# Seven-product pairs in half of the second feed-forward's down projections

## The chip, the core and the metric

The kernel runs on one core of a Trainium2 chip. Five engines work side by side, each through its own list of instructions in order: TensorE (PE: matmuls; the loading of its stationary operand is shown as PEld), VectorE (DVE), ScalarE (ACT), GpSimd (POOL) and SyncE (SP), which here only issues transfers. Engines wait for each other through semaphores. The metric is the time of one execution on the device, in microseconds; the kernel before takes 2179.33 us (median of three runs, 2179.05 to 2179.38).

## The reference

One decoder layer on 256 tokens with 16 learned tokens ahead of them, model width 2048, all in float32. The part that is changed is the last one:

```
gate, up = split(rms_norm(s) @ w_gu)          # 2048 -> 2 x 5632
s = s + 0.5 * ((silu(gate) * up) @ w_down)    # 5632 -> 2048, the "down projection"
out = rms_norm(s)[:, 16:]
```

`w_down` is 5632 x 2048. Ahead of this stand a first feed-forward of the same kind, an attention branch and a convolution branch with gates, and an output projection.

## The kernel before

**Split operands.** Each float32 operand of a matmul is made into two parts of the type float32r: `hi`, a rounded copy made on ACT, and `lo`, the rest, made on DVE by a subtraction. A product of two operands is three matmuls, hi x hi, lo x hi and hi x lo. For weights the parts are called `wh` and `wl`. `parts` (L407) makes them: a cast on ACT at L420 and a subtraction on DVE at L421, for 128x1024 (a tile) or 128x512 elements. PE reads `wl` only in the third matmul of a product. A tile's buffers, `wh` and `wl`, come from three each (`W_BUFS`), so a tile can be split as soon as the third tile before it has been used. A 512-wide tile takes two buffers of another pair, "sc", which has two.

**Order of the work.** `step` (L252) holds each tile's matmuls back until `AHEAD` = 2 more tiles have had their splitting written down. So in DVE's list the splits of the next two tiles stand ahead of the steps that evict a finished sum. The final order on each engine is made by a planner, which keeps to this order where the operands allow it and fills gaps with later work; buffers of one pool go to tiles in the order in which the program names them. Three lists carry side work: `pending` (evictions, run by `flush`), `later` (the `back` steps) and `side` (other small jobs); stages pop them at fixed tiles.

**Two ways of a matrix product.** `linear_tok` (L345) multiplies 256 tokens (two halves, i) by 1024 columns (two blocks of 512, q), going through the rows of the weight in chunks of 128: 2 x 2 products of three matmuls, 12 per chunk, 24 per pair of chunks, into four accumulators. `linear_mix` (L498) goes through pairs of chunks, with a letter for each in its plan. A D pair is as in `linear_tok`: 24 matmuls into the accumulators 2, 3, 4 and x. An S pair does the same 2x2 block product with seven products in place of eight (Winograd's form of Strassen's scheme): 21 matmuls into the accumulators 1 to 7. For that it needs sums of blocks of the weight (`sums`, L550: t13 by one 128x1024 addition at L553, t24 by two 128x512 additions at L554 and L555), and four sums of blocks of the activation, split into parts (`combine`, L483). t13 can also be made by two transfers, the second of which adds (`prefetch`, L559, issued by POOL at L563 and L564); the pairs for which that is done are the fourth entry of a plan. The third entry says after which tile the weight sums of which pair are made; the second entry is the pair at which `later` is popped. The result has to be put together from the seven accumulators when they are finished (`done`).

**The second feed-forward.** The 5632 inner columns are 11 groups of 512. They are done in thirds of 4, 4 and 3 groups. In each third, `gate_up_mix` makes the group's gate and up columns by `linear_mix` (plan `FFN2`, "DDSDSSDS", for the first group `FFN2_FIRST`) and turns the product with four PE transposes per `back` step (L647) into the activation `m`, already split. Then the down projection of this third's rows adds to `sT`, the residual, kept by token, in two stages of 1024 columns: u=0 and u=1. Both are `linear_tok`, of 16 chunks in the first two thirds and 12 in the last. Their four accumulators are evicted at the second chunk of the next stage by L1058, which halves and adds. In the last third the eviction also squares and sums each row (L1062) and multiplies by the last norm's gain (L1064); the very last stage holds back the second token half of its last six chunks (`HOLD`), so that the first half can be finished early.

**Buffers that the change touches.** `aux` has three buffers. The gate/up groups use them for t13 (`prefetch` into them runs ahead as far as they are free); the branch gates' stage (plan `GATES`, "DDDSDSDS", no t13 by transfer) holds its activation sums in them.

The accumulators lie in eight banks. Weights come on SP's queue into four staging buffers `st`, 1 MB for a pair.

Of the kernel before, what the change touches and what calls it, by code (L numbers as in the profile page):

```python
# [22 lines left out]
GC = 4  # L23
GW = GC * P
W2 = D // 2
# [14 lines left out]
HOLD = 6  # L40
# [3 lines left out]
GATES = ("DDDSDSDS", 2, {(2, 1): 3, (4, 1): 5, (6, 1): 7}, ())  # L44
FFN2_FIRST = ("DDDDSSDS", 1, {(3, 0): 4, (3, 1): 5, (6, 0): 7}, (4, 5))
FFN2 = ("DDSDSSDS", 1, {(1, 1): 2, (3, 0): 4, (3, 1): 5, (6, 0): 7}, (2, 4, 5))
AHEAD = 2


@with_exitstack  # L50
def decoder_layer(ctx: ExitStack, tc: tile.TileContext, t, out):
    nc = tc.nc
# [11 lines left out]
    def wide(shape, name):  # L64
        return tmp.tile(shape, F32, tag="wide", bufs=4, name=name)
# [16 lines left out]
    x = t["x"][0]  # L82
# [25 lines left out]
    def load_vectors():  # L108
# [12 lines left out]
        out=mask[:, T - P :],  # L121
# [330 lines left out]
    class Mixed:  # L452
# [22 lines left out]
        def sum(self, p):  # L475
# [4 lines left out]
                nc.vector.tensor_scalar_mul(f[:, k, :], s(c, NMETA), col(self.g0 + c))  # L480
            self.combine(p, f)

        def combine(self, p, f):  # L483
            a11, a12, a21, a22 = (f[:, c, i * P : (i + 1) * P] for i in range(2) for c in range(2))
            q = tmp.tile([P, 4, P], F32, tag="sc", name="sums")
            nc.vector.tensor_sub(q[:, 0, :], a21, a22)
            nc.vector.tensor_sub(q[:, 1, :], q[:, 0, :], a11)
            nc.vector.tensor_sub(q[:, 2, :], a11, a21)
            nc.vector.tensor_add(q[:, 3, :], a12, q[:, 1, :])
            sp = (aux if self.in_aux else apool).tile([P, 4, 2, P], F32R, tag="act", name=f"sp{p}")  # L490
            nc.scalar.copy(out=sp[:, :, 0, :], in_=q)
            nc.vector.tensor_sub(sp[:, :, 1, :], q, sp[:, :, 0, :].bitcast(F32))
            self.sums[p] = [[sp[:, k, lo, :] for lo in range(2)] for k in range(4)]
# [4 lines left out]
    def linear_mix(plan, a, w, cols, name, done):  # L498

# [36 lines left out]
        def load(p):  # L536

            st = wpool.tile([P, 2, 2, GW], F32, tag="st", bufs=ST_BUFS, name="st")
            rows = w[2 * p * P : (2 * p + 2) * P, :].rearrange("(c p) f -> p c f", p=P)
            for q in range(2):  # L540
                nc.sync.dma_start(out=st[:, :, q, :], in_=rows[:, :, cols[q] : cols[q] + GW])
            if kinds[p] == "S":
                if not by_load:
                    t13s[p] = wpool.tile([P, 2, GW], F32, tag="tt", bufs=2, name="t13")
                elif p not in by_load:
                    t13s[p] = aux.tile([P, 2, GW], F32, tag="act", name="t13")
                t24s[p] = wpool.tile([P, 2, GW], F32, tag="tt", bufs=2, name="t24")
            return st
# [176 lines left out]
    for half in halves:  # L725
# [288 lines left out]
    def finish_part(i):  # L1014

        nc.vector.tensor_reduce(out=fr[:, i, 3:4], in_=fss[:, i, 0:3], axis=AX.X, op=ALU.add)
        nc.vector.tensor_scalar(fpart[:, i : i + 1], fr[:, i, 3:4], 1.0 / D, EPS, op0=ALU.mult, op1=ALU.add)

    def finish(i, last):

        ms, a, r, n = (fr[:, i, k : k + 1] for k in range(4))
        nc.vector.tensor_scalar(ms, fss[:, i, 3:4], 1.0 / D, fpart[:, i : i + 1], op0=ALU.mult, op1=ALU.add)
        nc.scalar.activation(a, ms, AF.Sqrt)
        nc.vector.reciprocal(r, a)
        nc.vector.scalar_tensor_tensor(out=n, in0=r, scalar=ms, in1=r, op0=ALU.mult, op1=ALU.mult)
        nc.vector.tensor_scalar(n, n, -0.5, 1.5, op0=ALU.mult, op1=ALU.add)
        nc.vector.tensor_mul(a, r, n)
        rows = out[i * P : (i + 1) * P, :]
        for u, q in ((0, 1), (0, 0), (1, 0), (1, 1)) if i else ((0, None), (1, None)):
            cs = slice(0, W2) if q is None else slice(q * GW, (q + 1) * GW)  # L1030
            on_act = q == 0 or (q is None and u == 0)
            y = last if u and q else sT[i][u][:, cs]
            if on_act:
                nc.scalar.mul(y, y, a)
            else:
                nc.vector.tensor_scalar(y, y, r, n, op0=ALU.mult, op1=ALU.mult)
            eng = nc.scalar if on_act and i else nc.sync
            eng.dma_start(out=rows[:, u * W2 + cs.start : u * W2 + cs.stop], in_=y)

    w_gu, w_down = t["ffn2_w_gu"][0], t["ffn2_w_down"][0]  # L1040
    thirds = [list(range(0, 4)), list(range(4, 8)), list(range(8, ng))]
    for half in thirds:
        m = Act("m", len(half) * GC, SEQ)
        for gi, g in enumerate(half):
            gate_up_mix(FFN2 if g else FFN2_FIRST, hn, norm3, w_gu, g, m, gi)
        final = half is thirds[-1]
        if final:
            for q in range(2):
                nc.gpsimd.dma_start(
                    out=gfin[q],  # L1050
                    in_=t["norm_final"][q * W2 : (q + 1) * W2].rearrange("(o d) -> o d", o=1).to_broadcast([P, W2]),
                )
        for u in range(2):

            def down(i, q, ps, u=u, final=final):
                fs = slice(q * GW, (q + 1) * GW)
                v = sT[i][u][:, fs]
                nc.vector.scalar_tensor_tensor(out=v, in0=ps, scalar=0.5, in1=v, op0=ALU.mult, op1=ALU.add)  # L1058
                if final:
                    k = u * 2 + q  # L1060
                    sq = wide([P, GW], "fsq")
                    nc.scalar.activation(sq, v, AF.Square, accum_out=fss[:, i, k : k + 1])  # L1062
                    y = wide([P, GW], "fy") if k == 3 and i else v
                    nc.vector.tensor_mul(y, v, gfin[u][:, fs])  # L1064
                    if k == 1 and i:

                        nc.scalar.activation(fr[:, i, 3:4], fss[:, i, 1:2], AF.Sqrt)
                    if k == 2:
                        finish_part(i)
                    if k == 3:  # L1070
                        finish(i, y)

            hold = HOLD if final and u else 0
            linear_tok(
                [(m, 0, w_down, u * W2 + q * GW) for q in range(2)], list(range(len(half) * GC)), half[0] * GC, "pd",
                down if hold else lambda acc, down=down: [down(i, q, acc[i][q]) for q in range(2) for i in range(2)],
                hold=hold,
            )
    drain()


# [23 lines left out]
```

## Time and profile before

The profiled execution took 2179.22 us, of which the instructions span 2177.4. Its engines:

| | busy us | share of the span |
|---|---|---|
| PE matmuls | 2166.5 | 99% |
| weight loads (beside PE) | 1966.7 | 90% |
| DVE | 1485.7 | 68% |
| ACT | 1060.8 | 49% |
| POOL | 64.8 | 3% |

The stretches of the second feed-forward, by where the product names on PE change (us from the span's start):

| stretch | from | to | us |
|---|---|---|---|
| first third, down u=0 | 1635.71 | 1680.20 | 44.49 |
| first third, down u=1 | 1680.20 | 1723.72 | 43.52 |
| fifth gate/up group | 1723.72 | 1765.30 | 41.58 |
| second third, down u=0 | 1890.04 | 1934.53 | 44.49 |
| second third, down u=1 | 1934.53 | 1978.06 | 43.53 |
| last third, down u=0 | 2102.57 | 2136.18 | 33.61 |
| last third, down u=1, up to where `HOLD` works off its last block | 2136.18 | 2168.86 | 32.68 |

How to read the lines in this document: a timeline row is start, duration, engine, line of the kernel, operation, result<-operands, shape; "[1.20 <-ACT wh L420]" is idle time of that engine just before, and what ended it. "pd" are the down projection's accumulators, "pg" and "g" those of the gate/up groups and the branch gates, "t" the sums of weights, "sums" and "sp" those of the activation, "mt_ps" and L652 the transposes of `back`. A stretch's row gives its length, then the busy time of PE, PEld, DVE, ACT and POOL, the granted clock of PE, the share of the transfer engines and GB/s.

### The profile page before, as it was taken

The numbers are of one execution on the slowest core, as the hardware profiler recorded it, in microseconds if no ns is written. First come the engines' busy times: TensorE is split into PE (matmuls) and PEld (weight loads), VectorE is DVE, ScalarE is ACT, GpSimd is POOL, SyncE is SP. The second block draws the span as 40 slices with busy tenths as digits, with TensorE's granted clock in tenths as the row PEclk, the third lists the DMA queues.
The fourth block names the chain that finished last, engine by engine and source line by source line (L and its number), as shares of the span: only waits on it lengthen the run. The fifth ranks groups of instructions, "written<-read, shape, count | busy, mean of one in ns | idle before, by whom it ended". The sixth has DMA issues, their size and how long they took to land.

```text
span 2177.4 us, 33253 instructions
## 1 busy us (share of the span) xinstructions
PE 2166.5 (99%) x13489; PEld 1966.7 (90%) x13489; DVE 1485.7 (68%) x1942; ACT 1060.8 (49%) x1333; POOL 64.8 (3%) x73
## 2 busy tenths in 40 slices
PE   9999999999999999999999999999999999999998
PEld 9999999999999999999988888888888888888886
DVE  8555554445555555567897778678996599957985
ACT  6343343343433444444555555456664466534654
POOL 0000000000000000000000000001110011100100
PEclk9999999999999999999999999999999999999999
DMA  7555555555555555444555556557887589866973
GB/s 254 174 175 175 174 178 174 175 175 175 175 175 173 175 175 185 162 154 139 173 186 204 191 201 224 194 191 241 265 271 234 190 280 278 272 209 207 288 241 116
DMA packets 206432, 435.52 MB, mean 200 GB/s; under 512 B 10237, under 2 KB 10950, under 8 KB 206278
## 3 DMA queue, kind: packets, MB, share of 16 engines
q1 hardware_dynamic: 192214, 398.13, 53.4%
q0 software_dynamic: 13600, 34.61, 6.8%
q8 instruction: 105, 1.72, 0.3%
q10 hardware_dynamic: 464, 0.66, 0.1%
q14 instruction: 49, 0.40, 0.1%
HBM read 431.26 MB, written 2.10 MB: 199 GB/s over the span
## 4 chain that ended last, share of the span: by engine, by line
PE 98%; DVE 1%; ACT 0%; DMA 0%; issue 0%; SPq 0%; DVEq 0%
PE pg L518 6%; PE pg L519 6%; PE pg L520 6%; PE pd L320 4%; PE pu L320 4%; PE pd L318 4%; PE pu L318 4%; PE pu L319 4%; PE pd L319 4%; PE pg L320 4%; PE pg L318 4%; PE pg L319 4%; PE pd L360 4%; PE pd L359 4%; PE pd L358 4%; PE o L316 3%
## 5 line engine op out<-in xcount | busy, mean ns | idle before, releaser
L307 DVE TENSOR_TENSOR wl<-st,wh 128x1024 fp32r<-128x1024 f32 (+1 forms) x393 | 479.4, 1221 | 439.5 <-ACT wh L302 438.7
L302 ACT CAST wh<-st 128x1024 fp32r<-128x1024 f32 (+1 forms) x392 | 410.7, 1048 | 604.0 <-PE pd L319 147.3
L421 DVE TENSOR_TENSOR wl<-st,wh 128x1024 fp32r<-128x1024 f32 (+1 forms) x360 | 408.6, 1140 | 132.4 <-ACT wh L420 130.9
L420 ACT CAST wh<-st 128x1024 fp32r<-128x1024 f32 (+1 forms) x360 | 347.6, 986 | 260.6 <-PE pd L359 121.3
L318 PE MATMUL pg<-h,wh 128*128 128x272 f32 x704 | 203.2, 289 | 1.0 <-ACT h L190 0.7
L318 PE MATMUL pu<-h,wh 128*128 128x272 f32 x704 | 203.1, 289 | 0.0
L318 PE MATMUL pd<-m,wh 128*128 128x272 f32 x704 | 203.1, 288 | 0.0
L320 PE MATMUL pd<-m,wl 128*128 128x272 f32 x704 | 203.0, 288 | 0.0
L320 PE MATMUL pu<-h,wl 128*128 128x272 f32 x704 | 203.0, 288 | 0.0
L319 PE MATMUL pu<-h,wh 128*128 128x272 f32 x704 | 202.4, 288 | 0.0
L319 PE MATMUL pd<-m,wh 128*128 128x272 f32 x704 | 202.4, 288 | 0.0
L319 PE MATMUL pg<-h,wh 128*128 128x272 f32 x704 | 201.9, 288 | 0.1
L320 PE MATMUL pg<-h,wl 128*128 128x272 f32 x704 | 201.1, 289 | 0.3
L420 ACT CAST wh<-t 128x1024 fp32r<-128x1024 f32 x110 | 115.3, 1052 | 145.0 <-DVE t L555 82.9
L421 DVE TENSOR_TENSOR wl<-t,wh 128x1024 fp32r<-128x1024 f32 x110 | 134.2, 1223 | 37.7 <-ACT wh L420 32.8
L519 PE MATMUL pg<-wh,h 128*128 128x512 f32 x399 | 156.3, 392 | 0.0
L520 PE MATMUL pg<-wl,h 128*128 128x512 f32 x399 | 156.1, 391 | 0.0
L518 PE MATMUL pg<-wh,h 128*128 128x512 f32 x399 | 155.7, 390 | 0.0
L358 PE MATMUL pd<-wh,m 128*128 128x512 f32 x352 | 137.5, 391 | 0.0
L360 PE MATMUL pd<-wl,m 128*128 128x512 f32 x352 | 137.1, 389 | 0.0
L359 PE MATMUL pd<-wh,m 128*128 128x512 f32 x352 | 137.0, 389 | 0.0
L318 PEld LDWEIGHTS pg<-h,wh 128*128 128x128 f32 x704 | 132.3, 188 | 1.9 <-ACT h L190 0.9
(297 smaller groups left out, 4787.7 us busy)
## 6 DMA issues: line engine op xcount, KB each, us to landing
st<-in_ffn_w_gu_dram SPq DMA_DIRECT2D x183, 512.0 KB, 5.4
st<-in_ffn_w_down_dram SPq DMA_DIRECT2D x88, 1024.0 KB, 5.1
st<-in_ffn_w_gu_dram SPq DMA_DIRECT2D x84, 1024.0 KB, 4.9
st<-in_w_in_dram SPq DMA_DIRECT2D x48, 1024.0 KB, 5.1
st<-in_w_gate_dram SPq DMA_DIRECT2D x64, 512.0 KB, 4.3
t<-in_ffn_w_gu_dram POOLq DMA_DIRECT2D x64, 512.0 KB, 7.4
st<-in_w_branch_dram SPq DMA_DIRECT2D x32, 512.0 KB, 4.9
st<-in_w_out_dram SPq DMA_DIRECT2D x16, 1024.0 KB, 5.1
```

The costliest lines, as they stand in the source:

```text
L302: nc.scalar.copy(out=wh[:, :m, :], in_=sw)
L307: nc.vector.tensor_sub(wl[:, :m, :], sw, wh[:, :m, :].bitcast(F32))
L318: nc.tensor.matmul(a, wh[:, i, f], act.part(c, 0, t0, t1), start=first, stop=False)
L319: nc.tensor.matmul(a, wh[:, i, f], act.part(c, 1, t0, t1), start=False, stop=False)
L320: nc.tensor.matmul(a, wl[:, i, f], act.part(c, 0, t0, t1), start=False, stop=last)
L358: nc.tensor.matmul(ps, hi, wh[:, q, :], start=first, stop=False)
L360: nc.tensor.matmul(ps, hi, wl[:, q, :], start=False, stop=last)
L420: part_last[:] = [nc.scalar.copy(out=wh, in_=src).ins]
L421: part_last.append(nc.vector.tensor_sub(wl, src, wh.bitcast(F32)).ins)
L518: nc.tensor.matmul(ps[k], hi, wh, start=first, stop=False)
L519: nc.tensor.matmul(ps[k], lo, wh, start=False, stop=False)
L520: nc.tensor.matmul(ps[k], hi, wl, start=False, stop=left[k] == 0)
```

## The change

In one column half of each third the down projection goes by `linear_mix`, with S pairs.

- First two thirds: u=1 by `down_mix` with the plan `DOWN`, "DDSDSDSD": S pairs 2, 4 and 6 of 8. u=0 stays `linear_tok`, but at its chunks 3, 7 and 11 the sums of the activation for the pairs 2, 4 and 6 are made (`sum_of_parts`: hi and lo are added back together, then `combine`), into the three `aux` buffers.
- Last third: u=0 by `down_mix` with the plan `DOWN_LAST`, "DDDSDS": S pairs 3 and 5 of 6; their activation sums are made in the same stage, behind pairs 0 and 1, and the `back` steps of the last group at pair 1. u=1 stays `linear_tok` with `HOLD`.
- `t13` is made on DVE in both plans. The weight of a pair is loaded by one transfer, as in `linear_tok`.
- Evictions come as soon as an accumulator is finished, by the new `done`. In the last third squares and gain products (`score`) are made behind them, at the second chunk of u=1.

```diff
+DOWN = ("DDSDSDSD", None, {(1, 1): 2, (3, 1): 4, (5, 1): 6}, ())
+DOWN_LAST = ("DDDSDS", 1, {(2, 1): 3, (4, 1): 5}, ())
...
+        def sum_of_parts(self, p):
+
+            f = tmp.tile([P, 2, SEQ], F32, tag="sc", name="mf")
+            hi, lo = (self.act.tiles[p][:, :, k, :].bitcast(F32) for k in range(2))
+            nc.vector.tensor_add(f, hi, lo)
+            self.combine(p, f)
...
-            rows = w[2 * p * P : (2 * p + 2) * P, :].rearrange("(c p) f -> p c f", p=P)
-            for q in range(2):
-                nc.sync.dma_start(out=st[:, :, q, :], in_=rows[:, :, cols[q] : cols[q] + GW])
+            rows = w[(k0 + 2 * p) * P : (k0 + 2 * p + 2) * P, :].rearrange("(c p) f -> p c f", p=P)
+            if cols[1] == cols[0] + GW:
+                nc.sync.dma_start(out=st.rearrange("p c q f -> p c (q f)"), in_=rows[:, :, cols[0] : cols[0] + 2 * GW])
+            else:
+                for q in range(2):
+                    nc.sync.dma_start(out=st[:, :, q, :], in_=rows[:, :, cols[q] : cols[q] + GW])
...
+    def down_mix(plan, a, w, k0, u, end):
+        v = [[sT[i][u][:, q * GW : (q + 1) * GW] for q in range(2)] for i in range(2)]
+        ev = {}
+
+        def half_of(ps, out_, other, op1=ALU.add, by=0.5):
+            nc.vector.scalar_tensor_tensor(out=out_, in0=ps, scalar=by, in1=other, op0=ALU.mult, op1=op1)
+
+        def done(k, ps):
+            if k == "1":
+                ev["p1"] = wide([P, 2, GW], "dp")
+                nc.scalar.mul(ev["p1"][:, 0, :], ps, 0.5)
+                nc.vector.tensor_add(v[0][0], v[0][0], ev["p1"][:, 0, :])
+            elif k == "6":
+                half_of(ps, ev["p1"][:, 0, :], ev["p1"][:, 0, :])
+                nc.vector.tensor_add(v[1][0], v[1][0], ev["p1"][:, 0, :])
+            elif k == "5":
+                e = ev["p1"][:, 1, :]
+                half_of(ps, e, ev["p1"][:, 0, :], ALU.subtract)
+                for i in range(2):
+                    nc.vector.tensor_add(v[i][1], v[i][1], e)
+            elif k == "7":
+                half_of(ps, v[1][0], v[1][0])
+                half_of(ps, v[1][1], v[1][1], by=-0.5)
+            else:
+                i, q = {"2": (0, 0), "3": (0, 1), "4": (1, 0), "x": (1, 1)}[k]
+                half_of(ps, v[i][q], v[i][q])
+            ev[k] = True
+            if all(n in ev for n in "1234567x"):
+                pending.append(end)
+
+        linear_mix(plan, a, w, (u * W2, u * W2 + GW), "pd", done, k0)
...
+            if final and u == 0:
+                side.append(lambda: None)
+                side.extend(lambda p=p: ma.sum_of_parts(p) for p in (3, 5))
+                down_mix(
+                    DOWN_LAST, ma, w_down, half[0] * GC, u,
+                    lambda score=score: [score(i, q) for q in range(2) for i in range(2)],
+                )
+            elif u == 0:
+                side.append(lambda: None)
+                side.extend(lambda p=p: ma.sum_of_parts(p) for p in (2, 4, 6))
+                linear_tok(
+                    ops, chunks, half[0] * GC, "pd",
+                    lambda acc, down=down: [down(i, q, acc[i][q]) for q in range(2) for i in range(2)],
+                    side_at=(3, 7, 11),
+                )
+            elif not final:
+                down_mix(DOWN, ma, w_down, half[0] * GC, u, lambda: None)
+            else:
+                linear_tok(ops, chunks, half[0] * GC, "pd", down, hold=HOLD)
```

`score` is the part of the old `down` that followed the eviction (L1059 to L1071), unchanged. The empty first entry of `side` is taken by the last tile of the gate group, whose matmuls are written down after it.

More of the change, by code (lines that the diff above doesn't have):

```diff
@@ L1068, in down @@
[L1068 to L1078, printed above, removed]
+                    score(i, q)
@@ new lines, in decoder_layer @@
+            ops = [(m, 0, w_down, u * W2 + q * GW) for q in range(2)]
+            chunks = list(range(len(half) * GC))
+            if final and u == 0:
[17 more added lines that the diff above has]
+                linear_tok(ops, chunks, half[0] * GC, "pd", down, hold=HOLD)
```

26 lines of the change are left out of this document (16 added, 10 removed).

## The prediction

> **What bounds the kernel now.** I read the page from the top: busy times first, then the chain that ended last. The reader should see that TensorE (PE) is busy from end to end and is nearly the whole chain, so the time is the sum of its work, and only work taken from PE, or a gap put into it, moves the time.
>
> ```profile
> span 2177.4 us, 33253 instructions
> PE 2166.5 (99%) x13489; PEld 1966.7 (90%) x13489; DVE 1485.7 (68%) x1942; ACT 1060.8 (49%) x1333; POOL 64.8 (3%) x73
> PE 98%; DVE 1%; ACT 0%; DMA 0%; issue 0%; SPq 0%; DVEq 0%
> ```
>
> Next the busy times by stretch, cut where the product names change. They are, in order: the first third's down projections, column half u=0, then u=1; one gate/up group (plan with four S pairs); the last third's u=0; one stage of the branch gates (`GATES`, three S pairs). Columns: length, then PE, PEld, DVE, ACT, POOL busy, granted clock, DMA share. PE is busy for the whole of each at clock 1.00, and VectorE (DVE) is far from full in the down stages (21.9 of 43.5) but near it where S pairs run (34.8 of 42.5).
>
> ```profile
> 1635.71:1680.20 44.49, 44.49 (x201) 36.83 (x200) 27.10 (x29) 18.48 (x20) 1.17 (x1) 1.00 0.74 233
> 1680.20:1723.72 43.52, 43.52 (x193) 36.05 (x192) 21.91 (x21) 16.88 (x17) 0.00 (x0) 1.00 0.58 194
> 1723.72:1765.30 41.58, 41.58 (x185) 34.36 (x184) 34.72 (x39) 25.13 (x28) 4.69 (x5) 1.00 0.75 230
> 2102.57:2136.18 33.61, 33.61 (x154) 27.81 (x152) 22.20 (x25) 15.36 (x18) 0.00 (x0) 1.00 0.59 188
> 1309.78:1352.29 42.51, 42.51 (x193) 35.14 (x192) 34.78 (x37) 22.89 (x27) 4.01 (x4) 1.00 0.70 232
> ```
>
> The profile's 0.39 us is a matmul's passage, not its price: matmuls overlap. The PE timeline has the price, the distance of two starts.
>
> ```profile
> 1635.71 0.39 PE L358 MATMUL pd<-wh,m 128*128 128x512 f32 x1
> ...
> 1636.39 0.39 PE L358 MATMUL pd<-wh,m 128*128 128x512 f32 x1
> ```
>
> Three matmuls in 0.68 us are 0.2267 us each; 192 of them make 43.52, the second stretch exactly. The first has two `back` steps besides: 0.97 us, 0.48 each.
>
> **The change part by part.** (1) *Matmuls removed.* A D pair is 24 matmuls, an S pair 21. `DOWN` has three S pairs and runs twice, `DOWN_LAST` has two and runs once: 8 pairs x 3 x 0.2267 = **-5.44 us**. Everything else is on engines beside PE, so it costs only where PE has to wait. PE waits for `wl`, the last thing made for a tile, and that is DVE's. DVE's prices, from the groups by shape and from the sums' tile:
>
> ```profile
> L421 DVE TENSOR_TENSOR wl<-st,wh 128x1024 fp32r<-128x1024 f32 x305 | 371.6, 1222 | 132.4 <-ACT wh L420 130.9
> L554 DVE TENSOR_TENSOR t<-t,st 128x512 f32<-128x512 f32 x55 | 37.7, 685 | 0.0
> L1058 DVE SCALAR_TENSOR_TENSOR sT<-pd,sT 128x512 f32<-128x512 f32 x24 | 16.1, 687 | 15.8 <-PE pd L360 15.8
> L488 DVE TENSOR_TENSOR sums<-sf x4: 280/284/286, 1427.7 to 1476.0; 128x128 f32<-128x128 f32 x4
> L491 ACT CAST sp<-sums x7: 617/620/622, 1089.0 to 1477.9; 128x512 fp32r<-128x512 f32 x7
> ```
>
> As with PE, starts are nearer than durations. This is DVE at the end of a `GATES` stage; PE starts the next stage at 1352.29:
>
> ```profile
> 1348.27 1.23 DVE L421 TENSOR_TENSOR wl<-t,wh 128x1024 fp32r<-128x1024 f32 x1 [1.20 <-ACT wh L420]
> 1349.70 1.23 DVE L421 TENSOR_TENSOR wl<-t,wh 128x1024 fp32r<-128x1024 f32 x1 [0.21 <-ACT wh L420]
> 1350.84 0.68 DVE L615 TENSOR_TENSOR cgate<-g,cup 128x512 f32<-128x512 f32 x1
> 1351.44 1.22 DVE L421 TENSOR_TENSOR wl<-st,wh 128x1024 fp32r<-128x1024 f32 x1
> ...
> 1355.51 0.68 DVE L625 TENSOR_TENSOR cgate<-g,cgate 128x512 f32<-128x512 f32 x1
> 1356.11 0.68 DVE L622 TENSOR_TENSOR cup<-cup,u2x 128x512 f32<-128x512 f32 x1
> 1356.71 1.22 DVE L421 TENSOR_TENSOR wl<-st,wh 128x1024 fp32r<-128x1024 f32 x1
> ...
> 1358.44 0.68 DVE L626 TENSOR_TENSOR cup<-cup,g 128x512 f32<-128x512 f32 x1
> 1359.04 2.35 DVE L421 TENSOR_TENSOR wl<-st,wh 128x1024 fp32r<-128x1024 f32 x2
> ```
>
> So a 1024-wide split is 1.13 and a 512-wide step 0.60 from start to start; for a 128-wide one I take 0.20 (its 0.28 less the same 0.08). The Trainium skill, in "VectorE: DVE Perf Modes", section "The DRAIN you can't avoid", says that the next operation waits until the pipe has emptied. Read so, each step would cost its whole duration; these rows start the next one 0.08 to 0.09 earlier, and the rows decide.
>
> (2) *Sums of the activation in u=0 of the first two thirds.* Three steps of one add 0.6, four small ones 0.8, one split 0.6 = 2.0 us of DVE and 0.62 of ScalarE (ACT): 6 us onto 27.1 of 44.49. Cost **0**, hidden by DVE's idle 17 us. They move past nothing on SP; what POOL has behind them is rival D.
>
> (3) *The S pairs inside `DOWN`.* Against two tiles of a D pair, an S pair has one of 512 and three of 1024 plus 1.13 + 0.6 + 0.6 for the weights' sums: 6.3 us of DVE in 21 x 0.2267 = 4.76 of PE; with its D pair 8.6 in 10.2. That is the `GATES` stage's own rhythm, sums of weights on DVE included, and that stage's 42.51 us is 183 x 0.2267 + 0.97 = 42.46. Cost **0** there. The load is one transfer of 1 MB on SP as before, same bytes. The start has only two D pairs (10.9 us of PE) for four splits 4.5, four evictions 2.4 and weight sums 2.3 = 9.2: it fits.
>
> (4) *The end of `DOWN`.* "1", "6", "5" and "7" need eight DVE steps after the last S pair, as many as in `GATES`. There the first tile of the next stage is split by 1352.66 and wanted at 1352.74, and PE slips:
>
> ```profile
> 1352.74 0.47 PE L360 MATMUL z<-wl,ya 128*128 128x512 f32 x1
> 1353.05 0.39 PE L358 MATMUL z<-wh,yc 128*128 128x512 f32 x1
> ```
>
> 0.31 instead of 0.23: 0.08 lost. Then "2", "3", "4", "x" (2.4 us) stand ahead of the fifth split, which in `GATES` ends at 1361.39 and is wanted at 1352.29 + 10.88 + 0.08 + 0.45 = 1363.7 (a tile's third matmul, 2 x 0.2267 in, is the first to read `wl`): 0.1 late. **+0.2 each, +0.4** for both, between 0 and 1.0 each.
>
> (5) *`DOWN_LAST`, its first S pair.* Its stage takes over a DVE that is already behind with the last gate group:
>
> ```profile
> 2108.33 1.22 DVE L421 TENSOR_TENSOR wl<-st,wh 128x1024 fp32r<-128x1024 f32 x1
> 2109.47 1.41 DVE L639 SCALAR_TENSOR_TENSOR cup<-cup,rtok,cgate 128x512 f32<-128x512 f32 x2
> 2110.79 2.35 DVE L421 TENSOR_TENSOR wl<-st,wh 128x1024 fp32r<-128x1024 f32 x2
> 2114.50 1.23 DVE L421 TENSOR_TENSOR wl<-st,wh 128x1024 fp32r<-128x1024 f32 x1 [1.36 <-ACT wh L420]
> ```
>
> From 2110.79 on there is now: sum of pair 3 (2.0), two splits (2.26), two `back` splits (1.2), weight sums (2.33), sum of pair 5 up to its four small steps (1.4): 9.2, so 2120.0. The sum's last split (0.6) and pair 3's first split (0.6) follow, since both use the two "sc" buffers: 2121.2 at the densest, 2122.2 if one more split slips in while ACT copies. PE wants it at 2102.57 + 6 x 2.72 + 0.97 + 0.45 = 2120.3. **+1.4** (0.9 to 1.9; 0 if the order lets pair 3 take its buffers before the sum of pair 5).
>
> (6) *`DOWN_LAST`, its end, into u=1.* All but "x" finish in the last S pair. Against (4) that puts "3" and "1" (1.2 us) ahead of the next stage's first split, less the 0.21 idle: 1.0 late. "6" has a second step: the third split, wanted at 1358.3 and ended at 1357.93 in `GATES`, is then 1.6 - 1.0 - 0.35 = 0.25 later. "x" fits the idle 1.20. **+1.3** (0.3 to 2.0). The squares and products of `score` come later, where before they came with the evictions; the tail with HOLD is the same.
>
> Sum: -5.44 + 0.4 + 1.4 + 1.3 = **-2.3 us** on the profiled run's 2179.22 (1.8 us around its span); the median of the runs is 2179.33, so **2177.0**. What is late after that is DVE again, never PE.
>
> **The rivals.** *A: the saving in full.* The list of steps is ordered so that splits go first and the stalls of (5) and (6) vanish: 2179.33 - 5.44 + 0.4 = 2174.3. For it: in the rows of (1) a split stands between the two steps for "7" (L625, L626), so order bends to need. Against: DVE has no idle time from 2108 to 2113 to bend into.
>
> *B: nothing left.* (4) to (6) at their upper ends, 2.0 + 1.9 + 2.0 = 5.9: 2179.8. Against: it needs all three.
>
> *C: DVE paced by durations.* If each step cost 0.09 more, the S/D rhythm would be 8.6 us plus nine steps x 0.09 plus the two waits of 1.20 and 0.21: 10.8 in 10.2, 0.6 lost per S pair of `DOWN`, 3.6 in all; (5) would grow by 1.5 and (6) by 1.1: 2177.0 + 6.2 = 2183.2. Against: the `GATES` stage, same rhythm, loses nothing. The skill's rule above is this rival.
>
> *D, slower: the t13 prefetch late.* The sums now hold the three "aux" buffers that the next third's gate group prefetches into from POOL. That POOL waits for such readers the trace shows:
>
> ```profile
>   PE g L520: 1333.5, 2
> ```
>
> In the old kernel a prefetch's two halves and the reading steps of the group that begins at 1723.72 were:
>
> ```profile
> 1633.63 0.76 POOL L563 DMA_DIRECT2D t<-in_ffn_w_gu_dram  x1 [1.62 <-DVE wl L421]
> 1642.81 1.17 POOL L564 DMA_DIRECT2D t<-in_ffn_w_gu_dram  x1 [8.42 <-DMA t<-in_ffn_w_gu_dram]
> DMA to landing us min/median/max: 5.6/8.7/10.5
> 1741.21 0.69 DVE L554 TENSOR_TENSOR t<-t,st 128x512 f32<-128x512 f32 x1
> ```
>
> The last buffer is free when pair 6 is done, 1680.20 + 36.04 = 1716.2; with 9.2 to the second half and 8.7 to land that is 1734.1, against a reader of the last prefetched pair at 1741.21 - 2.0 = 1739.2. 5.1 us to spare. It decides only if the landing slips by more than that; 9 us later costs 4 in each of two groups: 2185.
>
> **How the numbers follow.** My forecast 0.58, A 0.25, B 0.09, C 0.03, D 0.05. 0.2% is 4.36 us, about what a measurement tells from no change: below 2174.97 is faster, above 2183.69 slower. A and the lucky edge of the forecast give faster 0.27; D and the upper half of C slower 0.07; the rest, 0.66, is same. The range 2174.0 to 2179.8 runs from A to B and leaves out C and D and edges; the forecast's own is 2175.2 to 2178.6.
>
> **What would show it.** Right: the stretch of each `DOWN` 2.0 us shorter; PE gaps of some 1 us after `DOWN_LAST`'s third pair and at the start of the last stage, waiting on `wl`; DVE near 90% busy in `DOWN`. No such gaps: A. Gaps inside `DOWN` at each S pair: C. DVE waiting on a DMA before L554's step in the fifth or ninth gate group: D. Wrong altogether if PE waits for banks, or if the order of steps moves elsewhere.

## The result and the profile after

The changed kernel takes 2175.79 us (median of 20 runs, 2175.61 to 2176.11), the kernel before on the same chip 2179.15 (2178.90 to 2180.73). The ratio is 0.9984 with a 95% interval of 0.9977 to 0.9991: a gain of 3.4 us or 0.15%, real, and within the 0.2% that the prediction counted as the same. The forecast was 2177.0, a gain of 2.3, in a range of 2174.0 to 2179.8.

The page of the profiled execution (2176.08 us) starts like this:

```profile
span 2174.3 us, 33362 instructions
PE 2162.1 (99%) x13465; PEld 1961.7 (90%) x13465; DVE 1546.9 (71%) x2054; ACT 1078.0 (50%) x1360; POOL 64.6 (3%) x73
PE 97%; DVE 2%; ACT 0%; issue 0%; DMA 0%; SPq 0%; DVEq 0%
```

PE is still the chain, with 13465 records of matmuls in place of 13489, the 24 that the S pairs save. DVE has 61.2 us more to do, and one thing is new in the chain: 2% of it is DVE in place of 1%. To find the place, the PE timeline is cut where the product names change, as before:

| stretch | before | after | difference |
|---|---|---|---|
| first third's down projections | 88.01 | 86.03 | -1.98 |
| gate/up groups of the second third | 166.32 | 166.60 | +0.28 |
| second third's down projections | 88.01 | 86.03 | -1.98 |
| gate/up groups of the last third | 124.51 | 124.77 | +0.26 |
| last third's, up to the last matmul's start | 66.03 | 66.26 | +0.23 |
| last matmul's start to the end | 8.85 | 8.84 | -0.01 |

The two `DOWN` give their nine matmuls each almost whole (9 x 0.2267 = 2.04). Each gives some 0.27 back in the stage behind it. The last third loses: six matmuls fewer should have saved 1.36, and it got 0.23 longer, so 1.59 went into stalls there.

By stretch (length, then PE, PEld, DVE, ACT, POOL busy, clock, DMA share), first third's u=0 and u=1, then the last third, cut at 2131.50, about where `DOWN_LAST` ends:

```profile
1635.77:1680.26 44.49, 44.49 (x201) 36.83 (x200) 32.93 (x47) 20.04 (x24) 0.00 (x0) 1.00 0.59 189
1680.26:1721.80 41.54, 41.54 (x184) 34.36 (x183) 35.55 (x40) 21.57 (x24) 4.63 (x5) 1.00 0.81 246
2099.20:2131.50 32.30, 32.30 (x147) 26.56 (x146) 32.30 (x47) 18.57 (x23) 0.00 (x0) 1.00 0.55 185
2131.50:2165.50 34.00, 32.80 (x145) 26.77 (x143) 27.17 (x41) 17.56 (x29) 0.00 (x0) 1.00 0.29 103
```

u=0 with the sums takes 44.49 as it did before. In `DOWN` DVE is busy 35.55 of 41.54 and PE never waits. In `DOWN_LAST` DVE is busy for all of the 32.30, and still PE is too. Only the last row has PE short of its length, by 1.20. The list of waits of PE from 2099 to the end has one entry, and the PE timeline has its place:

```profile
PE pd L362 <- DVE wl L423: 1.2, 1, 1.2
```

```profile
2138.55 0.39 PE L361 MATMUL pd<-wh,m 128*128 128x512 f32 x1
2140.14 1.19 PE L362 MATMUL pd<-wl,m 128*128 128x512 f32 x4 [1.20 <-DVE wl L423]
```

(Lines are those of the changed kernel: L423 is the split's subtraction, L422 its cast, L360 to L362 the products of `linear_tok`, L527 to L529 those of `linear_mix`, L1059 `half_of`, L1065, L1068 and L1073 the additions for "1", "6" and "5".) From start to start it is 1.59 in place of 0.23: 1.36 lost. What DVE did ahead of it:

```profile
2131.21 1.22 DVE L423 TENSOR_TENSOR wl<-st,wh 128x1024 fp32r<-128x1024 f32 x1
2132.34 0.68 DVE L1059 SCALAR_TENSOR_TENSOR sT<-pd,sT 128x512 f32<-128x512 f32 x1
2132.94 0.68 DVE L1059 SCALAR_TENSOR_TENSOR dp<-pd,dp 128x512 f32<-128x512 f32 x1
2133.54 1.22 DVE L423 TENSOR_TENSOR wl<-st,wh 128x1024 fp32r<-128x1024 f32 x1
2134.68 0.69 DVE L1068 TENSOR_TENSOR sT<-sT,dp 128x512 f32<-128x512 f32 x1
2135.28 0.68 DVE L1059 SCALAR_TENSOR_TENSOR dp<-pd,dp 128x512 f32<-128x512 f32 x1
2135.88 0.68 DVE L1059 SCALAR_TENSOR_TENSOR sT<-pd,sT 128x512 f32<-128x512 f32 x1
2136.48 1.29 DVE L1073 TENSOR_TENSOR sT<-sT,dp 128x512 f32<-128x512 f32 x2
2137.68 1.28 DVE L1059 SCALAR_TENSOR_TENSOR sT<-pd,sT 128x512 f32<-128x512 f32 x2
2138.88 2.35 DVE L423 TENSOR_TENSOR wl<-st,wh 128x1024 fp32r<-128x1024 f32 x2
```

The splits at 2131.21 and 2133.54 are for the first two tiles of u=1. The third starts at 2138.88, after seven eviction steps (from 2134.68 on) without a split between them. They are 4.2 us of work on accumulators that nobody waits for, ahead of a split that PE waits for.

The smaller loss comes behind each `DOWN`, on PE at the first tile of the gate group that follows (here the first `DOWN`), for which DVE makes `wl` late, behind its evictions:

```profile
1721.80 0.39 PE L527 MATMUL pg<-wh,h 128*128 128x512 f32 x1
1722.03 0.39 PE L528 MATMUL pg<-wh,h 128*128 128x512 f32 x1
1722.36 0.50 PE L529 MATMUL pg<-wl,h 128*128 128x512 f32 x1
1722.70 0.40 PE L527 MATMUL pg<-wh,h 128*128 128x512 f32 x1
```

```profile
1721.09 1.22 DVE L423 TENSOR_TENSOR wl<-st,wh 128x1024 fp32r<-128x1024 f32 x1
```

Twice 0.33 or 0.34 in place of 0.227: 0.22. The split ends at 1722.31, and L529, the first to read it, was due at 1722.26.

### The profile page after: what moved, and what is told of

Read it like the earlier page. It is cut to its first block, busy times and chain, and to the rows that moved or that the text cites. A ratio compares the mean times of both kernels' runs of the same rounds, so it can differ in the third digit from the quotient of the medians.

```text
span 2174.3 us, 33362 instructions
## 1 busy us (share of the span) xinstructions
PE 2162.1 (99%) x13465; PEld 1961.7 (90%) x13465; DVE 1546.9 (71%) x2054; ACT 1078.0 (50%) x1360; POOL 64.6 (3%) x73
## 4 chain that ended last, share of the span: by engine, by line
PE 97%; DVE 2%; ACT 0%; issue 0%; DMA 0%; SPq 0%; DVEq 0%
PE pg L529 6%; PE pg L527 6%; PE pg L528 6%; PE pd L322 4%; PE pu L322 4%; PE pd L320 4%; PE pu L320 4%; PE pd L321 4%; PE pu L321 4%; PE pg L322 4%; PE pg L320 4%; PE pg L321 4%; PE o L318 3%; PE g L527 2%; PE g L528 2%; PE g L529 2%
## 5 line engine op out<-in xcount | busy, mean ns | idle before, releaser
L423 DVE TENSOR_TENSOR wl<-st,wh 128x1024 fp32r<-128x1024 f32 (+1 forms) x360 | 403.3, 1126 | 71.3 <-ACT wh L422 69.5
L422 ACT CAST wh<-st 128x1024 fp32r<-128x1024 f32 (+1 forms) x360 | 342.7, 976 | 209.9 <-PE z L361 38.1
L422 ACT CAST wh<-t 128x1024 fp32r<-128x1024 f32 x126 | 131.5, 1051 | 175.7 <-DVE t L567 116.4
L423 DVE TENSOR_TENSOR wl<-t,wh 128x1024 fp32r<-128x1024 f32 x126 | 153.2, 1222 | 41.1 <-ACT wh L422 36.1
L529 PE MATMUL pg<-wl,h 128*128 128x512 f32 x399 | 156.4, 392 | 0.0
L528 PE MATMUL pg<-wh,h 128*128 128x512 f32 x399 | 156.3, 392 | 0.0
L527 PE MATMUL pg<-wh,h 128*128 128x512 f32 x399 | 155.8, 390 | 0.0
L320 PEld LDWEIGHTS pg<-h,wh 128*128 128x128 f32 x704 | 132.2, 188 | 1.9 <-ACT h L192 1.0
L321 PEld LDWEIGHTS pg<-h,wh 128*128 128x128 f32 x704 | 132.7, 189 | 0.3 <-DVE h L193 0.3
L321 PEld LDWEIGHTS pu<-h,wh 128*128 128x128 f32 x704 | 132.7, 188 | 0.0
L321 PEld LDWEIGHTS pd<-m,wh 128*128 128x128 f32 x704 | 132.7, 189 | 0.0
```

Of the source, the lines that this page charges most:

```text
L320: nc.tensor.matmul(a, wh[:, i, f], act.part(c, 0, t0, t1), start=first, stop=False)
L321: nc.tensor.matmul(a, wh[:, i, f], act.part(c, 1, t0, t1), start=False, stop=False)
L422: part_last[:] = [nc.scalar.copy(out=wh, in_=src).ins]
L423: part_last.append(nc.vector.tensor_sub(wl, src, wh.bitcast(F32)).ins)
L527: nc.tensor.matmul(ps[k], hi, wh, start=first, stop=False)
L528: nc.tensor.matmul(ps[k], lo, wh, start=False, stop=False)
```

## The experiments

Two theories were set against each other. S: the loss is one stall at `DOWN_LAST`'s end, made by the order in DVE's list. R, the rival: it is DVE's load, spread over the stages with S pairs, and shows wherever DVE happens to be behind. Ratios are to the kernel before on the same chip. Diffs are against the changed kernel unless said.

### The new form in the first two thirds alone

```diff
             if final and u == 0:
-                side.append(lambda: None)
-                side.extend(lambda p=p: ma.sum_of_parts(p) for p in (3, 5))
-                down_mix(
-                    DOWN_LAST, ma, w_down, half[0] * GC, u,
-                    lambda score=score: [score(i, q) for q in range(2) for i in range(2)],
+                linear_tok(
+                    ops, chunks, half[0] * GC, "pd",
+                    lambda acc, down=down: [down(i, q, acc[i][q]) for q in range(2) for i in range(2)],
                 )
```

> The first two thirds as in the changed kernel, the last third as in the kernel before. Theory S (the saving lost is DOWN_LAST's own: its six matmuls, 1.36 us, are eaten by the PE gap of 1.36 us at 2138.55 and some small ones): DOWN keeps 2 x 2.04 less 0.22 at each of its two ends, so 3.6 us under the kernel before, at or a little below the changed kernel. Rival R (the loss is spread over the stage ends of DOWN and over DVE in general): only some 2.0 us under the kernel before, 1.3 above the changed kernel.

Measured: 2176.25 us (2175.92 to 2176.66), ratio 0.9987 (0.9978 to 0.9996), 2.8 us less than before's 2179.04 and between the two expectations. In the trace S holds: both down stretches are 86.03, the last third is 66.03 as in before, and PE's last matmul starts at 2164.83, 3.76 us earlier than in before; 0.29 of that was there already when the first third's down projections began (1635.42 against 1635.71), so the changed stages and the groups behind them give 3.47. But from there to the end it takes 9.57 us where the others take 8.85. That was looked at in a run of its own.

### The same once more

The same kernel, no edit.

> The kernel with the new form in the first two thirds alone, unchanged, once more: its PE ended 3.76 us earlier than before's, but its span only 3.0 us, because the last output transfer took 5.4 us from its issue to the end where before and the changed kernel show 4.7. If that is the transfer's own scatter, the profile now shows some 4.7 and a span near 2173.7, and the median lies at 2175.6 to 2176.3. If something in this kernel delays it, it is 5.4 again with a span of 2174.4.

Measured: 2176.23 us (2176.17 to 2176.41), span 2174.5; the delay is there again, so it is the kernel's and not scatter. From the last output transfer's issue to the end of the span (transfers of the last 8 us, the changed kernel first, then this one):

```profile
out_dram<-fy SPq DMA_DIRECT2D x1, 256.0 KB, 3.2
```

```profile
q14 instruction: 1, 0.01, 0.2%
out_dram<-fy SPq DMA_DIRECT2D x1, 256.0 KB, 3.9
```

The last transfer lands 0.7 us later, and a packet of an instruction queue, q14, moves in that time. Of the eleven profiles of this case only the two of this kernel show such a packet there, and only these two have the late landing. That goes together; that the packet delays the transfer was not tested apart. Without these 0.7, the gain would be some 3.5, near S's 3.6.

### The new form in the last third alone

```diff
-            elif u == 0:
-                side.append(lambda: None)
-                side.extend(lambda p=p: ma.sum_of_parts(p) for p in (2, 4, 6))
+            elif not final:
                 linear_tok(
                     ops, chunks, half[0] * GC, "pd",
                     lambda acc, down=down: [down(i, q, acc[i][q]) for q in range(2) for i in range(2)],
-                    side_at=(3, 7, 11),
                 )
-            elif not final:
-                down_mix(DOWN, ma, w_down, half[0] * GC, u, lambda: None)
```

> The last third as in the changed kernel, the first two thirds as before. Theory S: within 0.3 us of the kernel before (1.36 saved, 1.4 lost in the gap in the last stage, which is there again). Rival R: 1.36 us under the kernel before, with no gap over 1 us.

Measured: 2179.24 us (2178.97 to 2179.47), ratio 1.0000 (0.9992 to 1.0009). The last third is 66.25, and PE's only wait of it is the same, 1.2 us for `wl` at the third tile of u=1. `DOWN_LAST` gains nothing by itself: its 1.36 are what its end costs.

### The sums alone

Against the kernel before: `sum_of_parts` at the chunks 3, 7 and 11 of u=0 in the first two thirds, the sums not used, both halves by `linear_tok`.

```diff
...
+                side.append(lambda: None)
+                side.extend(lambda p=p: ma.sum_of_parts(p) for p in (2, 4, 6))
                 linear_tok(
                     ops, chunks, half[0] * GC, "pd",
                     lambda acc, down=down: [down(i, q, acc[i][q]) for q in range(2) for i in range(2)],
+                    side_at=(3, 7, 11),
                 )
...
```

> The kernel before with the activation sums of the first two thirds made in u=0 (the side steps at chunks 3, 7 and 11), but no S pair: nobody reads them. Theory S and the prediction: 0.0 us against the kernel before, within 0.3, since 6 us of DVE per third lie in its idle time. Rival: each sum holds up a split and PE shows gaps behind chunks 3, 7, 11: 0.5 us or more slower.

Measured: 2178.97 us (2178.85 to 2179.39), ratio 0.9999 (0.9990 to 1.0009), all stretches as in before. The sums are free.

### `DOWN_LAST`'s evictions put off

```diff
-    def down_mix(plan, a, w, k0, u, end):
+    def down_mix(plan, a, w, k0, u, end, late=""):
...
-        linear_mix(plan, a, w, (u * W2, u * W2 + GW), "pd", done, k0)
+        def done_late(k, ps):
+            if k in late:
+                pending.append(lambda: done(k, ps))
+            else:
+                done(k, ps)
+
+        linear_mix(plan, a, w, (u * W2, u * W2 + GW), "pd", done_late, k0)
...
                     DOWN_LAST, ma, w_down, half[0] * GC, u,
                     lambda score=score: [score(i, q) for q in range(2) for i in range(2)],
+                    late="6457",
```

> The changed kernel, but in the last third the evictions of the accumulators 6, 4, 5 and 7 are put off to the second chunk of the last stage, behind the splits of its first tiles. The number of steps on DVE is the same, only their order differs. If the gap comes from the order (eight evictions ahead of the third tile's split): the gap goes, 1.3 to 1.4 us under the changed kernel, about 2174.4. If it comes from DVE's total load: the gap moves to the fourth or fifth tile and at most 0.4 us is won.

Measured: 2174.33 us (2174.04 to 2174.52), ratio 0.9978 (0.9969 to 0.9987), 1.5 us less than the changed kernel. PE has no wait left in the list from 1635 on. DVE, and the same two stretches of the last third:

```profile
2132.82 3.64 DVE L423 TENSOR_TENSOR wl<-st,wh 128x1024 fp32r<-128x1024 f32 x3
2136.39 0.68 DVE L1059 SCALAR_TENSOR_TENSOR dp<-pd,dp 128x512 f32<-128x512 f32 x1
```

```profile
2099.09:2131.39 32.30, 32.30 (x147) 26.56 (x146) 32.30 (x47) 18.56 (x23) 0.00 (x0) 1.00 0.55 183
2131.39:2163.83 32.44, 32.44 (x145) 26.84 (x143) 27.25 (x41) 17.56 (x29) 0.00 (x0) 1.00 0.29 110
```

Three splits now stand ahead of the eviction of "6". DVE has the same work, 32.30 + 27.25 = 59.55 us against 59.47, and as many instructions; PE loses nothing. It was the order, not the load: S holds, and R falls for this stall.

### `DOWN_LAST` ending in a D pair

```diff
-DOWN_LAST = ("DDDSDS", 1, {(2, 1): 3, (4, 1): 5}, ())
+DOWN_LAST = ("DDSDSD", 1, {(1, 1): 2, (3, 1): 4}, ())
...
-                side.extend(lambda p=p: ma.sum_of_parts(p) for p in (3, 5))
+                side.extend(lambda p=p: ma.sum_of_parts(p) for p in (2, 4))
```

> The changed kernel with DOWN_LAST as DDSDSD (S pairs 2 and 4 of 6, sums for 2 and 4) in place of DDDSDS: as many matmuls, evictions and sums, but the stage ends in a D pair and the first S pair comes 5.4 us earlier. If the 1.36 us lost in the last stage come from the order (eight eviction steps in DVE's list ahead of the third tile's split), they go: last third 64.8 to 65.0 us instead of 66.26, about 2174.5. If a late start counts, as step (5) of the prediction said, it shows here: pair 2's first wl is wanted 5.4 us earlier, behind the same last gate group's steps on DVE, a gap of 2 to 4 us ahead of its matmuls and about 2177.5. If both hold, 2176 to 2177.

Measured: 2176.85 us (2176.42 to 2178.47), ratio 0.9990 (0.9981 to 0.9999), 1.1 us more than the changed kernel's 2175.79. Both halves of the text hold: the gap in u=1 is gone, and two others came, one in each S pair. PE's waits from 2098 on, and the places:

```profile
PE pd L527 <- ACT wh L422: 1.1, 1, 1.1
PE pd L527 <- ACT sp L500: 0.8, 1, 0.8
```

```profile
2113.58 0.72 PE L527 MATMUL pd<-wh,sp 128*128 128x512 f32 x2 [0.75 <-ACT sp L500]
2125.02 0.50 PE L527 MATMUL pd<-wh,sp 128*128 128x512 f32 x1 [1.10 <-ACT wh L422]
```

Start to start they are 1.14 and 1.50, 0.92 + 1.28 = 2.2 lost, less than the 2 to 4 us at pair 2 alone that were expected. PE waits first for the activation's sum itself, which DVE makes behind the last gate group's steps. The second wait is for the cast of a sum of weights: DVE ends that sum at 2123.82 and ACT casts it from 2123.93 on. So a late DVE at the start of the stage, the cause that step (5) of the prediction named, does count in this kernel, though what PE waits for is not the `wl` of the pair's first tile that the step had.

### Four additions on POOL

```diff
-    def down_mix(plan, a, w, k0, u, end):
+    def down_mix(plan, a, w, k0, u, end, add=nc.vector.tensor_add):
...
-                nc.vector.tensor_add(v[0][0], v[0][0], ev["p1"][:, 0, :])
+                add(v[0][0], v[0][0], ev["p1"][:, 0, :])
...
-                    nc.vector.tensor_add(v[i][1], v[i][1], e)
+                    add(v[i][1], v[i][1], e)
...
                     lambda score=score: [score(i, q) for q in range(2) for i in range(2)],
+                    add=nc.gpsimd.tensor_add,
```

> The changed kernel with the four additions of DOWN_LAST's evictions that read no accumulator (one for 1, one for 6, two for 5) made by POOL, which is idle there, in place of DVE. Four steps of 0.60, 2.4 us of DVE, leave the burst of eight. If the steps' number ahead of the third tile's split makes the gap of 1.36 us, it goes: about 2174.5. Against it: the steps for 6 and 5 rewrite what POOL reads, so DVE would wait for POOL; POOL's price for 128x512 is in no row here, and above some 1.2 us for one the wait takes the gain back: 2175.8 or more, with DVE waiting on POOL between 6 and 5.

Measured: 2178.09 us (2177.94 to 2178.35), ratio 0.9995 (0.9986 to 1.0004), 2.3 us more than the changed kernel. DVE (three rows of several) and POOL at the end of `DOWN_LAST`:

```profile
2131.45 0.69 DVE L1059 SCALAR_TENSOR_TENSOR sT<-pd,sT 128x512 f32<-128x512 f32 x1 [1.19 <-POOL sT L1065]
...
2136.20 0.69 DVE L1059 SCALAR_TENSOR_TENSOR sT<-pd,sT 128x512 f32<-128x512 f32 x1 [1.19 <-POOL sT L1068]
...
2141.11 0.69 DVE L1059 SCALAR_TENSOR_TENSOR sT<-pd,sT 128x512 f32<-128x512 f32 x1 [1.18 <-POOL sT L1073]
```

```profile
2129.39 2.03 POOL L1065 TENSOR_TENSOR sT<-sT,dp 128x512 f32<-128x512 f32 x1 [62.67 <-ACT dp L1064]
2133.96 2.20 POOL L1068 TENSOR_TENSOR sT<-sT,dp 128x512 f32<-128x512 f32 x1 [2.54 <-DVE dp L1059]
2137.57 3.52 POOL L1073 TENSOR_TENSOR sT<-sT,dp 128x512 f32<-128x512 f32 x2 [1.40 <-DVE dp L1059]
```

The four additions take 7.75 us on POOL, 1.9 each, about three times DVE's, and DVE, whose next evictions change the same part of `sT`, waits three times 1.19. Work given to an idle engine did not help, since it stayed in the same chain; PE waited 2.5 us in three places in place of 1.2 in one.

### S pairs in both halves, ending in an S pair

Against the kernel with the evictions put off: in the first two thirds u=0 goes by `down_mix` too, with the sums made there and kept for u=1, and evictions 6, 4, 5 and 7 put off in both.

```diff
-DOWN = ("DDSDSDSD", None, {(1, 1): 2, (3, 1): 4, (5, 1): 6}, ())
+DOWN_FIRST = ("DDDSDSDS", 1, {(2, 1): 3, (4, 1): 5, (6, 1): 7}, ())
+DOWN = ("DDDSDSDS", None, {(2, 1): 3, (4, 1): 5, (6, 1): 7}, ())
...
                 side.append(lambda: None)
-                side.extend(lambda p=p: ma.sum_of_parts(p) for p in (2, 4, 6))
-                linear_tok(
...
+                side.extend(lambda p=p: ma.sum_of_parts(p) for p in (3, 5, 7))
+                down_mix(DOWN_FIRST, ma, w_down, half[0] * GC, u, lambda: None, late="6457")
             elif not final:
-                down_mix(DOWN, ma, w_down, half[0] * GC, u, lambda: None)
+                down_mix(DOWN, ma, w_down, half[0] * GC, u, lambda: None, late="6457")
```

> The kernel with DOWN_LAST's evictions put off, and S pairs in u=0 of the first two thirds as well: both halves by down_mix with DDDSDSDS (S pairs 3, 5 and 7), the sums made once in u=0 and kept for u=1, evictions 6, 4, 5 and 7 put off to the next stage's first pair. Six more S pairs, 18 matmuls of 0.2267: -4.08 against 2174.33, so 2170.3 if nothing stalls, as the theory says that it is order and not DVE's load that costs. If DVE's load counts after all (S pairs through 87 us on end, behind a gate group), gaps at the first S pair of u=0 and in u=1: 1 us or more for each stage, 2172 to 2174. If the last sums' buffer, held 5.4 us longer than in the changed kernel, delays the t13 prefetch, gaps in the gate group that follows.

Measured: 2171.04 us (2170.79 to 2171.27), ratio 0.9962 (0.9949 to 0.9974), 8.0 us less than before's 2179.08. It is the fastest of the kernels run, 4.8 us under the changed one. The stretches u=0, u=1 and the gate group behind them:

```profile
1635.46:1677.90 42.44, 42.44 (x191) 34.53 (x190) 42.44 (x61) 23.95 (x30) 0.00 (x0) 1.00 0.58 192
1677.90:1720.00 42.10, 42.10 (x185) 34.45 (x185) 38.95 (x45) 21.97 (x25) 3.86 (x4) 1.00 0.74 236
1720.00:1761.60 41.60, 41.60 (x184) 34.27 (x183) 39.39 (x46) 24.92 (x28) 6.62 (x7) 1.00 0.94 277
```

DVE works through the whole of u=0 and PE has not one wait in the list. The two down stretches are 84.55 and 84.51 against 86.03, 1.5 shorter where nine matmuls should bring 2.04: the missing 0.5 are starts at 0.25 to 0.34 in a few places and many, some thirty of them at 0.234 to 0.240, a little above 0.227; what makes them late was not looked for. The gate groups behind `DOWN` lose their stall too (166.41 in place of 166.58, 124.52 in place of 124.79), and the first third's down projections begin 0.2 earlier. So the span falls by 3.7, from 2172.7 to 2169.0, against the 4.08 of the matmuls, the median by 3.3. The sums' last buffer, held some 5 us longer, delays no prefetch.

### S pairs in both halves, ending in a D pair

As the last one, but with "DDSDSDSD" in both halves, S pairs and sums 2, 4 and 6, and nothing put off there. The lines that are new against the changed kernel and not yet shown:

```diff
+DOWN_FIRST = ("DDSDSDSD", 1, {(1, 1): 2, (3, 1): 4, (5, 1): 6}, ())
...
+                side.extend(lambda p=p: ma.sum_of_parts(p) for p in (2, 4, 6))
+                down_mix(DOWN_FIRST, ma, w_down, half[0] * GC, u, lambda: None, late="")
...
```

> As the kernel with S pairs in both halves, but DDSDSDSD (S pairs 2, 4 and 6) in both and no eviction put off there (DOWN_LAST's are). As many matmuls: 2170.3 less nothing, plus 0.22 for each of the four ends in a D pair: 2170.8 if only order counts. The sum of pair 2 has to be made at the end of pair 0, right behind the last gate group: if the start counts, gaps of 2 to 4 us ahead of pair 2 in u=0 of both thirds, 2175 to 2178.

Measured: 2179.19 us (2178.70 to 2180.78), ratio 1.0001 (0.9992 to 1.0010). The same number of matmuls as in the fastest kernel, and 8.1 us more. PE's waits in the first third's down projections, and its rows at the larger (in this kernel the lines stand one further down, L424 for the split and L528 to L530 for the products):

```profile
PE pd L528 <- ACT wh L423: 1.8, 1, 1.8
PE pd L528 <- ACT sp L501: 0.8, 1, 0.8
```

```profile
1659.38 0.39 PE L529 MATMUL pd<-wh,m 128*128 128x512 f32 x1
1661.58 0.50 PE L528 MATMUL pd<-wh,sp 128*128 128x512 f32 x1 [1.81 <-ACT wh L423]
...
1663.46 0.63 PE L529 MATMUL pd<-wh,sp 128*128 128x512 f32 x1
1663.88 0.63 PE L528 MATMUL pd<-wh,sp 128*128 128x512 f32 x1
```

1.14 from start to start in the first S pair, for the activation's sum, and 2.20 in the second, for the cast of a sum of weights that DVE ends at 1660.37. In the fastest kernel, too, three sums are made in the first three pairs, right behind the last gate group, but there the first S pair is one D pair, 5.4 us, later; here DVE is not through with them. The two kernels differ also in what is put off, but almost nothing is lost behind `DOWN`: the down stretches of the first two thirds are 88.88 and 88.36 us in place of 84.55 and 84.51, the gate groups that follow 166.43 and 124.61 in place of 166.41 and 124.52. So the expected 0.22 for an end in a D pair did not come there. Behind the first `DOWN`, DVE and PE show:

```profile
1723.90 1.22 DVE L424 TENSOR_TENSOR wl<-st,wh 128x1024 fp32r<-128x1024 f32 x1
1725.52 0.61 PE L530 MATMUL pg<-wl,h 128*128 128x512 f32 x2
```

PE starts the gate group at 1724.39, so this split is later than in the changed kernel: 0.49 us ahead of the group in place of 0.71. But here five matmuls stand ahead of the first that reads it, not two, and no start is late. So here it is the order on PE that decides whether the end costs anything. What follows the second wait is told in the last section.

## Why the prediction was right or wrong

The forecast held in its range and its sign, with a gain that was 1.1 us too small. Against the profiled execution, 3.14 us less than before's, the terms stand like this:

| step | forecast | measured |
|---|---|---|
| (1) 24 matmuls | -5.44 | -5.44, of which 0.06 is lost in each `DOWN` |
| (2) sums in u=0 | 0 | 0 (44.49, and the run with the sums alone) |
| (3) S pairs inside `DOWN` | 0 | 0 |
| (4) both ends of `DOWN` | +0.4 | +0.54 |
| (5) `DOWN_LAST`'s first S pair | +1.4 | 0 |
| (6) `DOWN_LAST`'s end | +1.3 | +1.6 |
| sum | -2.3 | -5.44 + 0.12 + 0.54 + 1.6 = -3.2 |

The rest is 0.06 of a later start. Term (5) was 1.4 too high and the others together 0.6 too low, so a part of the nearness is luck.

**(1) to (4)** were right in kind and size. The `GATES` stage was a fair model for `DOWN`: the same rhythm of S and D pairs, and PE waits nowhere inside. At the end the first tile's split is late as foreseen, and costs 0.22 in place of 0.2; a few hundredths more are lost in the groups behind. The second part of that 0.2, at the fifth split, did not come. Nor is the loss bound to such an end: in the kernel with S pairs in both halves that ends in D pairs, PE's order avoids it.

**(5) failed.** The step put DVE's work in the order of the list and took pair 3's tiles in the order of the program: the 512-wide one first, its `wl` wanted after six tiles' matmuls. The changed kernel starts the stage 3.37 us earlier than before's, so the step's 2120.3, when it is wanted, is 2116.9 here, and the step's 2121.2, when its split ends, 2117.8. DVE was much later even than that; the split ends at 2121.94:

```profile
2121.25 0.69 DVE L423 TENSOR_TENSOR wl<-st,wh 128x512 fp32r<-128x512 f32 x1
```

But PE did not ask for it then. From the same trace, PE from 2116.49, where pair 3 begins:

```profile
2116.49 0.39 PE L527 MATMUL pd<-wh,m 128*128 128x512 f32 x1
...
2117.63 0.61 PE L529 MATMUL pd<-wl,m 128*128 128x512 f32 x2
...
2121.06 0.39 PE L527 MATMUL pd<-wh,m 128*128 128x512 f32 x1
...
2122.44 0.39 PE L529 MATMUL pd<-wl,sp 128*128 128x512 f32 x1
```

The planner took the late tile last, on both engines. The sum of pair 5 does stand ahead of it in DVE's list, as the step said, but so do the splits of the pair's three other tiles, from 2115.91 on, and one of pair 4's. PE begins pair 3 with the second tile, goes through the two with sums of weights, starts on pair 4 at 2121.06, and reads the 512-wide tile's `wl` only at 2122.44, 5.5 us later than the step had it; each start is still 0.23 or 0.24 behind the last. The step's lower bound had a bend only in DVE's list ("0 if the order lets pair 3 take its buffers before the sum of pair 5"); that PE can take the tiles of a pair in another order was left out. A late start does cost where the slack is smaller. With the first S pair one pair earlier, PE lost 0.92 in it and 1.28 in the next in `DOWN_LAST`; with such a start in the first two thirds, the whole gain.

**(6)** was right as a mechanism and wrong in the tile, and near in size partly by luck. The first tile of u=1 came in time, because PE's list again puts the first two matmuls of several products ahead of those that read `wl`, and the whole of the delay came at the third. In the program's order that tile's `wl` would be wanted at about 2131.50 + 5.44 + 0.45 = 2137.4, and its split, begun at 2138.88, ends at 2140.1: 2.7 us late, twice what the step had. PE's order hid the other half. Putting the evictions off takes the stall away with DVE's load unchanged.

**The rivals.** A, the saving in full at 2174.3 with splits ahead, had the stall of (5) right, which the order bent away although DVE had no idle time there, and that of (6) wrong. The same kernel with four evictions put off does what A says: 2174.33, a gain of 4.7 against A's 5.0. B needed (5). C, each step of DVE paced by its whole duration, would have shown gaps inside `DOWN`; the rule of the Trainium skill that stood beside it ("VectorE: DVE Perf Modes", section "The DRAIN you can't avoid") does not set the pace here: the two 512-wide steps of L1073 take 1.29 where 2 x 0.68 is 1.36, and steps after each other start 0.60 apart, as at 2134.68, 2135.28 and 2135.88. That section itself adds that a next operation that is not held starts earlier, which the prediction left out. D, the late prefetch, did not come, not even with the buffers held to the end of u=1.

The chances: 0.66 on a change that cannot be told from none by the 0.2% bound. The measured 0.15% lies there, though with twenty runs of each it can be told from none.

## What to carry to other kernels

When a stage on the bound engine gets shorter, look at its start and its end and not at its middle: here matmuls inside were saved almost to the last, and what was lost was lost where a burst of evictions stood ahead of the next stage's splits, or where sums had to be made right at the start. A helper engine that is busy all the time need cost little, if what the bound engine waits for stands first in its list (DVE was busy for all 42.44 us of a stage of the fastest kernel, and PE had no wait there); so try to put off the work that nobody waits for before moving it to another engine. And a deadline that is read off one engine's order holds only as long as that order can't bend: ask what else the bound engine could do first.

## What the runs showed of the hardware

**The clock after a wait.** In the kernel with S pairs in both halves that ends in D pairs, the wait of 1.81 us in the first third is followed by matmuls 0.42 to 0.43 us apart. One stretch of those:

```profile
1664.00:1665.00 1.00, 1.00 (x4) 0.81 (x3) 1.00 (x2) 1.00 (x2) 0.00 (x0) 0.50 0.00 0
```

The granted clock is 0.50 for some 3 us, and 1.00 again from 1668 on, which costs about 1.6 us more (seven starts at 0.427 in place of 0.227, with one of 0.396 ahead and one of 0.264 behind). The same wait in the second third, 2.19 from start to start, leaves the clock at 1.00; that third's down projections are still only 0.5 us shorter, as they have more short delays behind the wait. The Trainium skill ("TensorE: Matmul & The Clock Gate", section "What's actually happening") has the clock fall to half after an idle window of about 3.4 us, with a window that runs by itself and is not reset by the program. The half clock and the two outcomes of one wait agree with it; the length does not, since PE idled for only 1.8 us here.

**An instruction packet beside the last output.** In the kernel with the new form in two thirds alone, twice, the last transfer lands 3.9 us after its issue in place of 3.2, with a packet of an instruction queue in that time. The two go together in all eleven profiles; that the one causes the other was not tested.

**POOL beside DVE.** In the kernel with four additions on POOL, one 1024-wide split on DVE that ran while POOL was adding (2138.00, beside POOL's from 2137.57) took 1.93 us in place of 1.22:

```profile
2138.00 1.93 DVE L423 TENSOR_TENSOR wl<-st,wh 128x1024 fp32r<-128x1024 f32 x1
```

It is a single row: another split, at 2133.79, ran beside POOL's addition from 2133.96 and took 1.22. What slowed the one was not tested.
